# Forming the weight sums of five quads twice, in a projection kernel held by TensorE

## The chip, the cores and the metric

One core of a Trainium2 chip. The metric is the device time of one launch in microseconds, as the median of the runs shown.

## The reference

One layer of a hybrid decoder for 2048 new tokens of one sequence and 64 tokens of eight running ones (2112 rows of 1024 in all), in float32:

```python
xn = rms_norm(x, norm_pre)
z = einsum('btd,de->bte', xn, w_in)          # w_in: 1024 x 4096
v_pool, g_pool, u_lru, g_lru = four column blocks of z, 1024 wide each
y_pool = pool_mixer(v_pool)                  # causal means over 2/4/8/16 tokens, a 256x256 map per group, a scale
y_lru = rg_lru(causal_conv(u_lru))           # 4-tap convolution, two 128x128 gates per head, a linear scan over time
mixed = concat(y_pool * silu(g_pool), y_lru * silu(g_lru))
out = x + rms_norm(mixed @ w_out, norm_post)  # w_out: 2048 x 1024
```

Besides `out` the new states of the pool, the convolution and the scan are returned.

## The kernel before

**Tokens and quads.** The 2112 tokens are worked in three macro chunks of 704 (`m` = 0, 1, 2; `LM` = 2 is the last), each of two halves of 352. The 4096 columns of w_in are 16 quads per macro chunk, a quad `(m, p, kind)` being 256 columns: kind V (pool input), G (pool gate), U (lru input) or L (lru gate), p = 0 to 3. The order of p differs by macro chunk (`P_ORDER`); in the last third it is 1, 2, 3, 0. Every float32 operand is split into a high and a low part (fp32r), and a product takes three matmuls.

**Seven products for eight.** A quad is a 2 x 2 block product (two column blocks, two halves of the inner dimension) with two token halves. In the second and last third each quad is done with seven products in place of eight, the Strassen-Winograd way. The seven left operands carry numbers 1 to 7 (`pid`): 1, 2 and 4 are raw weight blocks ("11", "12", "22"), and 5, 7, 6, 3 are sums of them. The seven right operands are x or sums of x, and lie in `XN` under the names X11, T1, T2, X22, T3, X21, T4. One product is a *slot* of 12 matmuls of 352 columns in `quad_slot` (line 1127); the matmul's line is 267.

**Where weights come from.** All split operands of a quad go through tiles of one ring (`half_tile`, 7 buffers of 512 KB). A split operand is stored once to a DRAM scratch `wsd` by `hi_lo` (line 888, the store on line 898), and is read back by later macro chunks in `w_step` (line 980, load on line 984). In the second third a quad is *late* (`is_late`, line 763) if its sums do not exist yet: then `w_raw` (line 869) loads its four raw blocks (256 KB each, line 368) into the small rings `raw` and `tp`, `s_sum` (line 908) makes the sums in place on VectorE (lines 339 and 342), and each is cast on ScalarE (line 890) and subtracted on VectorE (line 339) into the ring, and stored. In the last third every operand is loaded from `wsd`.

**x for the next macro chunk.** `x_chain` (line 1415) loads token tiles (line 291) for the squares on ScalarE (line 307), then x itself, transposed, into the staging tiles `XA` and `XB` (line 1435), and scales it on VectorE (line 1457). `transition` (line 1471) then forms and splits the seven x operands out of the staging tiles.

**The order.** The program is written out by a planner: `one_slot` (line 1606) emits the matmuls of a slot and then, with `run_jobs`, whatever work of ScalarE ("A"), VectorE ("V") and GpSimd fits beside it by assumed durations; "t" in a job is a waiting time, "D" a DMA issue, "?" a condition. The result is one fixed order for each engine. Almost all DMAs are issued from the SyncE queue in the planner's order; the stores of `mixed` come from GpSimd. `prep` (line 1853) starts loads: raw blocks up to `RAW_AHEAD` = 14 slots before their quad, operands up to `AHEAD` = 6 slots. Each engine and each queue works in order, so an instruction that waits holds those behind it.

**After the projections.** `combos_chain` (line 1554) loads w_out, forms four sums of its blocks and stores them to DRAM (`wtd`), at a pace of 12 us for each of eight steps; `region_chain` (line 1579) loads and splits five pieces of w_out into tiles that take over the buffers of `XA` and `XB`, and spawns ahead of the sums. Both run during the last third. From about 805 us on the output projection runs over pairs of token tiles.

Of the kernel before, what the change touches and what calls it, by code (L numbers as in the profile page):

```python
# [25 lines left out]
LM = NM - 1  # L26
# [18 lines left out]
PIECE = 512  # L45
# [20 lines left out]
X0_LEAD = 3  # L66
FROM_P = 2
P_ORDER = ((0, 1, 2, 3), (2, 1, 3, 0), (1, 2, 3, 0))
TABLE_COST = 1.4
LAG = 4.0  # L70
WO_PACE = 12.0
# [1 line left out]
XL_ON = "V"  # L73
SG_ON = "V"
X_LEAD = (7, 10)
XOF_0 = {1: "X22", 5: "X11", 6: "T2", 3: "T4", 7: "T1", 2: "T3", 4: "A"}
ORDER_0 = (1, 5, 6, 3, 7, 2, 4)
XOF = {1: "X11", 6: "T2", 5: "T1", 7: "T3", 4: "T4", 2: "X21", 3: "X22"}
# [6 lines left out]
def hymba_kernel(  # L85
# [133 lines left out]
    def xa_tile(h, name, dtype=F32):  # L219
        return sb.tile([P, 2 * QW], dtype, tag=f"XA{h}", bufs=1, name=name)  # L220
# [143 lines left out]
    def blocks(kind, p):  # L364
        return [KINDS[kind] + 2 * p + j for j in range(2)]
# [392 lines left out]
    EARLY = "VG"  # L758

    def is_made(q):  # L760
        return q[0] == 0 and q[1] >= FROM_P and q[2] in EARLY

    def is_late(q):
        return q[0] == 1 and (q[1] < FROM_P or q[2] not in EARLY)

    w_tiles, w_rawt = {}, {}
    jobs, pe_q, clock, T = [], [], {"V": 0.0, "A": 0.0, "G": 0.0}, [0.0]
# [97 lines left out]
    PLAIN_PID = {"11": 1, "12": 2, "22": 4}  # L865
    S_OF = {5: "22", 6: "11", 7: "21", 3: "12"}
    w_time = {}

    def w_raw(q):
        _, p, kind = q  # L870
        w_time[q] = T[0] + 5.0
        for n in NAMES:
            blk, h = blocks(kind, p)[int(n[0]) - 1], int(n[1]) - 1
            t = (raw_tile if n[0] == "1" else tp_tile)(f"wr{q[0]}{kind}{p}_{n}")
            w_rawt[q, n] = w_load_raw(blk, h, t)

    def flat_of(t):
        return t.rearrange("p a b -> p (a b)")
# [9 lines left out]
    def hi_lo(hi, lo, src, store=None, key=None):  # L888
        yield "A", 0.62
        AC.copy(out=hi, in_=src)  # L890
        yield "V", 0.71
        tsub(lo, src, hi.bitcast(F32))
        if key:
            w_fin[key] = clock["V"] + HOP
        if store:
            yield "t", LAG
            yield "D", 0
            nc.sync.dma_start(out=w_key(*store[1:]), in_=store[0].bitcast(F32))

    w_jobs = {}  # L900
# [79 lines left out]
    def w_step(q, pid):  # L980
        m, p, kind = q
        t = w_tiles[q, pid] = half_tile(f"w{m}{kind}{p}_{pid}")
        if not is_late(q) or pid in (1, 2, 4):
            nc.sync.dma_start(out=flat_of(t).bitcast(F32), in_=w_key(kind, p, pid))
            return
        n = S_PID.index(pid)
        if n == 0:
            w_jobs[q, "s"] = {"n": 0, "job": spawn(s_sums(q, lambda i: w_jobs[q, "s"].update(n=i + 1)),
                                                        max(T[0], w_time[q]), rank=0,
                                                        due=lambda: w_first[q, S_PID[w_jobs[q, "s"]["n"]]] - 1)}  # L990
        box = w_jobs[q, "s"]

        def wait_split():
            yield "?", lambda: box["n"] > n
            yield from hi_lo(t[:, 0, :], t[:, 1, :], w_rawt[q, S_OF[pid]], (flat_of(t), kind, p, pid),
                             (q, pid))
        w_jobs[q, pid] = spawn(wait_split(), rank=0, due=lambda: w_first[q, pid])

    def need_w(q, n):
# [415 lines left out]
    def x_chain(m):  # L1415
        first = -(-m * MW // P)
        tiles = list(range(first, min(-(-(m + 1) * MW // P), N_TT)))
        places = [("B", 0), ("B", 1)] + ([("A", 0), ("A", 1)] if m > 1 else [])
        for i0 in range(0, len(tiles), len(places)):
            part = tiles[i0:i0 + len(places)]  # L1420
            for i, (s_, j) in zip(part, places):
                yield "D", 0
                load_tok(i, s_, j)
                yield "t", 3.0
            yield "t", 5.0
            for i in part:
                yield "A", 1.06
                tok_square(i)
        for h in (1, 0):
            if m == 1 and h == 0:  # L1430
                yield "?", lambda: x0_free
                x_tiles["A"] = xa_tile("A", "XA1")
            for k in range(0, HK, 2):
                yield "D", 0
                nc.sync.dma_start(out=stage_x(h)[:, k:k + 2, :],
                                  in_=xt[:, HK * h + k:HK * h + k + 2, m * MW:(m + 1) * MW])
                yield "t", 2.5
        yield "V", 0.2
        yield "A", 0.3, "sqrt"
        tok_rsqrt(tiles[0], tiles[-1] + 1)  # L1440
        clock["V"] = max(clock["V"], clock["A"]) + 0.5
        yield "t", 0.8
        yield "?", lambda: t_free() >= 2
        dg, rt = roots(m)
        for c in range(2):
            yield "A", 1.5
            r_diag(2 * m + c, dg[:, c * CW:(c + 1) * CW])
        for c in range(2):
            def rows(c=c):
                R = r_rows(2 * m + c, dg[:, c * CW:(c + 1) * CW])  # L1450
                return [("A", 0.45, lambda: AC.copy(out=rt[:, c * CW:(c + 1) * CW], in_=R))]
            yield "P", rows
        yield "t", 3.0
        for k in range(KT):
            yield "V", 0.92
            a = stage_x(k // HK)[:, k % HK, :]
            V.scalar_tensor_tensor(out=a, in0=a, scalar=col(C_NP, k), in1=rt[:, :MW], op0=ALU.mult, op1=ALU.mult)
        t_done(2)
        x_ready.add(m)
# [94 lines left out]
    def combos_chain():  # L1554
        def load(k):
            r = {}
            for i, j in ((0, 0), (1, 1), (0, 1), (1, 0)):
                r[i, j] = (raw_tile if i else tp_tile)(f"wo{k}_{i}{j}")
                nc.sync.dma_start(
                    out=r[i, j], in_=w_out[(8 * i + k) * P:(8 * i + k + 1) * P, PIECE * j:PIECE * (j + 1)])  # L1560
            return r
        nxt = load(0)
        yield "t", 6.0
        for k in range(KT):
            yield "D", 0
            r, nxt = nxt, load(k + 1) if k + 1 < KT else None
            for j, o, a, b in ((T1, (0, 0), (0, 1), (0, 0)), (T3, (0, 1), (1, 1), (0, 1)),
                               (T2, (1, 1), (1, 1), (0, 0)), (T4, (1, 0), (1, 0), (1, 1))):
                yield "V", 0.68
                tsub(r[o], r[a], r[b])  # L1570

                def store(j=j, k=k, o=r[o]):
                    yield "t", 2.0
                    yield "D", 0
                    nc.sync.dma_start(out=wtd[:, j, k, :], in_=o)
                spawn(store(), clock["V"] + HOP, rank=3)
            yield "t", WO_PACE

    def region_chain(r, j, k0, k1):
        yield "D", 0  # L1580
# [100 lines left out]
    with tc.manual_schedule():  # L1681
# [171 lines left out]
        def prep(n):  # L1853
            while raw_next[0] < len(raw_quads):
                q = raw_quads[raw_next[0]]
                if first_of[QUADS.index(q)] - n > RAW_AHEAD:
                    break
                if raw_next[0] > 1 and not raw_done(raw_quads[raw_next[0] - 2]):
                    break
                w_raw(q)  # L1860
                raw_next[0] += 1
            while w_next[0] < len(w_order):
                at, q, pid = w_order[w_next[0]]
                if at - n > AHEAD or (w_next[0] >= W_BUFS and w_last[w_order[w_next[0] - W_BUFS][1:]] > n):
                    break
                if (q[0] == 0 or is_late(q)) and q not in w_time:
                    break
                if q[0]:
                    w_step(q, pid)
                elif is_made(q):  # L1870
                    made_tile(q, pid)
                else:
                    plain_tile(q, pid)
                w_next[0] += 1
# [23 lines left out]
        for n, (qi, i, _, _) in enumerate(slots):  # L1898
            first_of.setdefault(qi, n)
        done = set()  # L1900
        first_made = min(qi for qi, q in enumerate(QUADS) if is_made(q))
        for n, (qi, i, qp, pid) in enumerate(slots):
            q = QUADS[qi]
# [15 lines left out]
                    0, ("X11", "T1", "T2", "A")[(len(x0_jobs) - 1) % 4]] - 2)  # L1919
            if m < LM and (qi, i) == (lasts[m] - X_LEAD[m], 0):  # L1920
                spawn(x_chain(m + 1), rank=0, due=lambda m=m: first_of[lasts[m]])
            if m == 2 and (qi, i) == (lasts[1] + 2, 0):
                spawn(region_chain(0, "b11", 0, 5), then=[lambda: spawn(combos_chain())])
                nc.sync.dma_start(out=stc, in_=st_conv)
                nc.sync.dma_start(out=stl, in_=st_lru)
            x_turn(n, qi)
# [23 lines left out]
        def p1_chain():  # L1950
# [10 lines left out]
            for g in range(5):  # L1961
                it = p1_slots(g)
                for part in range(3):
# [11 lines left out]
                            load_11(g + 4)  # L1975
                    yield [("A", 0.6, lambda g=g: p1_out(g))] if part == 2 else []

        spawn(region_chain(1, T3, 0, 8), rank=2)
        pc = p1_chain()
        for _ in range(15):  # L1980
# [132 lines left out]
```

## Time and profile before

| | us |
|---|---|
| median of 3 runs | 1149.36 |
| lowest and highest | 1147.45 and 1150.91 |
| profiled execution | 1153.73 |
| its span, first to last instruction | 1152.0 |
| second third of the tokens | about 293 to 547 |
| last third | about 547 to 805 |
| output projection | about 805 to the end |

In the profile PE is TensorE's matmul, PEld its weight load, DVE VectorE, ACT ScalarE, POOL GpSimd and SP SyncE. Tile names drop their numbers: `w1V` is a split weight operand of a V quad in the second third (`w2V`: last third), `wr1U` a raw block, `wsd` the scratch of split operands, `XAB` a staging tile of x, `lw` and `pw` the small maps, and `a1V`, `e1V`, `d1V` the three accumulators of a V quad in the second third. In rows of a timeline a bracket at the end gives the engine's idle time before the row and what ended it.

### The profile page before, as it was taken

How to read it: one execution, taken by the hardware profiler on the slowest of the kernel's cores; microseconds unless marked ns; L12 is line 12 of the kernel's file. 1: busy time of each engine (PE TensorE's matmuls, PEld its weight loads, DVE VectorE, ACT ScalarE, POOL GpSimd, SP SyncE). 2: the span in 40 equal slices, each digit the busy share in tenths (PEclk: the TensorE clock that was granted, in tenths of full speed). 3: DMA queues.
4: the chain of work that ended last, by engine and by line, in shares of the span. 5: the costliest groups of instructions: out<-in, count | busy, mean ns of one | idle time of the engine just before them, and what ended most of it. 6: DMA issues, size and time to landing. Idle time of an engine off the chain costs nothing. (4 is left out here: it accounts for less than half of the span.)

```text
span 1152.0 us, 17682 instructions
## 1 busy us (share of the span) xinstructions
PE 1119.7 (97%) x6226; PEld 1048.8 (91%) x6226; DVE 842.2 (73%) x1345; ACT 629.4 (55%) x1091; POOL 162.3 (14%) x264
## 2 busy tenths in 40 slices
PE   7999999999999989999999999999999999999996
PEld 5989999999999989999999999999888888888875
DVE  6798786768788657878787565645586678778777
ACT  4376778675676748458483636366663233344222
POOL 4200101002011100201011100201000012221232
PEclk9999999999999999999999999999999999999998
DMA  9655698885899998988999999987879567766553
GB/s 327 229 195 190 229 319 310 316 318 186 281 314 348 350 388 315 341 323 290 349 345 394 396 367 339 371 313 252 250 208 286 169 196 231 205 211 183 168 179 128
DMA packets 177464, 320.00 MB, mean 278 GB/s; under 512 B 24736, under 2 KB 86432, under 8 KB 177376
## 3 DMA queue, kind: packets, MB, share of 16 engines
q1 hardware_dynamic: 173536, 301.57, 76.4%
q0 software_dynamic: 3840, 17.30, 3.8%
q8 instruction: 49, 0.80, 0.3%
q14 instruction: 39, 0.32, 0.1%
HBM read 216.41 MB, written 102.15 MB: 277 GB/s over the span
## 5 line engine op out<-in xcount | busy, mean ns | idle before, releaser
L477 PE MATMUL p<-XN,s 128*128 128x512 f32 (+1 forms) x224 | 87.5, 391 | 2.1 <-DVE s L152 2.1
L475 PE MATMUL p<-XN,s 128*128 128x512 f32 (+1 forms) x224 | 87.4, 390 | 0.0
L476 PE MATMUL p<-XN,s 128*128 128x512 f32 (+1 forms) x224 | 87.3, 390 | 0.0
L1301 DVE SCALAR_TENSOR_TENSOR xs<-u,parT,xs 128x704 f32<-128x704 f32 (+1 forms) x72 | 66.8, 954 | 23.1 <-ACT xs L1290 22.9
L468 POOL TENSOR_TENSOR xr<-ac,xr 128x512 f32<-128x512 f32 x27 | 50.8, 1900 | 209.8 <-DVE ac L614 100.0
L269 PE MATMUL zL<-XN,wL 128*128 128x352 f32 x384 | 64.8, 325 | 0.6 <-DVE wL L339 0.6
L269 PEld LDWEIGHTS zL<-XN,wL 128*128 128x128 f32 x384 | 62.8, 188 | 0.8 <-DVE wL L339 0.8
L593 ACT ACTIVATE p<-ac 128x512 f32<-128x512 f32 (+1 forms) x32 | 18.8, 587 | 81.7 <-DVE ac L468 81.7
L468 DVE TENSOR_TENSOR a<-a,a 128x512 f32<-128x512 f32 x48 | 32.9, 690 | 37.2 <-DMA a<-mixed 34.5
L160 ACT ACT_TABLE_LOAD x46 | 59.0, 1283 | 1.5 <-PEq L2092 0.8
L149 ACT CAST s<-a 128x512 fp32r<-128x512 f32 x48 | 28.6, 616 | 53.5 <-DVE a L468 40.6
L1273 POOL DMA_DIRECT2D mixed<-g x24 | 13.2, 549 | 296.1 <-ACT g L1105 59.7
L476 PE MATMUL p<-XN,a 128*128 128x512 f32 x137 | 54.2, 396 | 0.0
L475 PE MATMUL p<-XN,a 128*128 128x512 f32 x137 | 54.2, 395 | 0.0
L477 PE MATMUL p<-XN,a 128*128 128x512 f32 x137 | 54.2, 395 | 0.0
L269 PE MATMUL y<-dh,pw 128*128 128x352 f32 x192 | 54.1, 323 | 0.0
L477 PEld LDWEIGHTS p<-XN,s 128*128 128x128 f32 x224 | 42.4, 189 | 12.1 <-DVE s L152 2.6
L476 PEld LDWEIGHTS p<-XN,s 128*128 128x128 f32 x224 | 42.5, 190 | 9.6
L475 PEld LDWEIGHTS p<-XN,s 128*128 128x128 f32 x224 | 42.5, 190 | 9.6
L269 PE MATMUL zU<-XN,wU 128*128 128x352 f32 x288 | 48.0, 325 | 0.0
L269 PEld LDWEIGHTS zU<-XN,wU 128*128 128x128 f32 x288 | 46.9, 188 | 0.0
L1264 DVE SCALAR_TENSOR_TENSOR g<-y,parT,g 128x352 f32<-128x352 f32 x48 | 27.9, 580 | 25.0 <-PE y L269 24.8
(407 smaller groups left out, 3140.4 us busy)
## 6 DMA issues: line engine op xcount, KB each, us to landing
a<-mixed SPq DMA_DIRECT2D x112, 256.0 KB, 4.1
mixed<-g POOLq DMA_DIRECT2D x48, 352.0 KB, 5.7
w2V<-wsd SPq DMA_DIRECT2D x28, 512.0 KB, 7.4
w2G<-wsd SPq DMA_DIRECT2D x28, 512.0 KB, 7.5
w2U<-wsd SPq DMA_DIRECT2D x28, 512.0 KB, 7.8
w2L<-wsd SPq DMA_DIRECT2D x28, 512.0 KB, 7.7
w1V<-wsd SPq DMA_DIRECT2D x20, 512.0 KB, 5.6
w1G<-wsd SPq DMA_DIRECT2D x20, 512.0 KB, 7.4
```

What stands on the lines that cost most here:

```text
L149: hi_eng.copy(out=hi, in_=src)
L160: nc.scalar.preload_act_table_set(name)
L269: nc.tensor.matmul(out, lhsT=lhsT, rhs=rhs, start=start, stop=stop)
L468: (eng or nc.vector).tensor_tensor(out=out, in0=a, in1=b, op=op)
L475: nc.tensor.matmul(out, lhsT=ah, rhs=wh, start=start and k == 0, stop=False)
L476: nc.tensor.matmul(out, lhsT=ah, rhs=wl, start=False, stop=False)
L477: nc.tensor.matmul(out, lhsT=al, rhs=wh, start=False, stop=stop and k == KT - 1)
L593: nc.scalar.activation(out=junk, in_=o, func=AF.Square, accum_out=st[:, g:g + 1])
L1264: V.scalar_tensor_tensor(out=g[:, cs], in0=Y, scalar=col(C_SCALE, blk), in1=g[:, cs], op0=ALU.mult, op1=ALU.mult)
L1273: nc.gpsimd.dma_start(out=mixed[:, blk, m * MW:(m + 1) * MW], in_=g[:, :MW])
L1301: V.scalar_tensor_tensor(out=xs, in0=E[:, k:k + n], scalar=col(C_CW + 8 * k, b), in1=xs, op0=ALU.mult, op1=ALU.add)
```

## The change

It has four parts.

1. `REMADE` names five quads: (1,"U"), (1,"L"), (2,"U"), (3,"U"), (3,"L"). In the last third they are late too: their four raw blocks are loaded again, now into the staging tiles of x (`XR1` to `XR5`, alternately in the buffers of `XB` and `XA`), and the sums 5, 7, 6 and 3 are formed and split again. Operands 1, 2 and 4 are still loaded from `wsd`. The sums of these quads are no longer stored in the second third. Raw loads of the last third wait until the transition to it is over (`x_jobs` empty).
2. The due time of the next sum is that of the earliest use among the sums not yet made, for all late quads.
3. The pace of the x loads is 3.0 us for the second third (before, 3.0 for tokens and 2.5 for x) and 7.0 for the last (before the same 3.0 and 2.5).
4. Since the raw blocks use the buffers of `XA` and `XB` until the last remade quad is done, `region_chain` is spawned only then, and `combos_chain` at its old place.

```diff
+REMADE = ((1, "U"), (1, "L"), (2, "U"), (3, "U"), (3, "L"))
...
+X_PACE = (3.0, 7.0)
...
     def is_late(q):
-        return q[0] == 1 and (q[1] < FROM_P or q[2] not in EARLY)
+        return q[0] == 1 and (q[1] < FROM_P or q[2] not in EARLY) or q[0] == 2 and q[1:] in REMADE
...
     def w_raw(q):
         _, p, kind = q
         w_time[q] = T[0] + 5.0
-        for n in NAMES:
+        if q[0] == LM:
+            n_xr[0] += 1
+            xr = xa_tile("AB"[n_xr[0] % 2], f"XR{n_xr[0]}")
+        for i, n in enumerate(NAMES):
             blk, h = blocks(kind, p)[int(n[0]) - 1], int(n[1]) - 1
+            if q[0] == LM:
+                w_rawt[q, n] = w_load_raw(blk, h, xr[:, PIECE * i:PIECE * (i + 1)])
+                continue
...
-                                                        due=lambda: w_first[q, S_PID[w_jobs[q, "s"]["n"]]] - 1)}
+                                                        due=lambda: min(w_first[q, o] for o in S_PID[w_jobs[q, "s"]["n"]:]) - 1)}
...
-            yield from hi_lo(t[:, 0, :], t[:, 1, :], w_rawt[q, S_OF[pid]], (flat_of(t), kind, p, pid),
-                             (q, pid))
+            store = None if (p, kind) in REMADE else (flat_of(t), kind, p, pid)
+            yield from hi_lo(t[:, 0, :], t[:, 1, :], w_rawt[q, S_OF[pid]], store, (q, pid))
...
                 load_tok(i, s_, j)
-                yield "t", 3.0
+                yield "t", X_PACE[m - 1]
...
-                yield "t", 2.5
+                yield "t", X_PACE[m - 1]
...
+                if q[0] == LM and (begun[0] < LM or x_jobs):
+                    break
                 w_raw(q)
...
+            if m == LM and not wo_begun and combos_done and raw_next[0] == len(raw_quads) and all(raw_done(q_) for q_ in raw_quads):
+                wo_begun.append(n)
+                spawn(region_chain(0, "b11", 0, 5))
             if m == 2 and (qi, i) == (lasts[1] + 2, 0):
-                spawn(region_chain(0, "b11", 0, 5), then=[lambda: spawn(combos_chain())])
+                spawn(combos_chain())
```

`combos_done` is set at the end of `combos_chain`.

More of the change, by code (lines that the diff above doesn't have):

```diff
@@ L867, in hymba_kernel @@
     w_time = {}
+    n_xr = [0]
     def w_raw(q):
@@ L1577, in combos_chain @@
             yield "t", WO_PACE
+        combos_done.append(True)
+    combos_done = []
     def region_chain(r, j, k0, k1):
@@ L1900, in hymba_kernel @@
         done = set()
+        wo_begun = []
         first_made = min(qi for qi, q in enumerate(QUADS) if is_made(q))
@@ L1976, in p1_chain @@
                     yield [("A", 0.6, lambda g=g: p1_out(g))] if part == 2 else []
+        assert wo_begun
         spawn(region_chain(1, T3, 0, 8), rank=2)
```

## The prediction

> **What bounds the kernel now.** I read the page first, then the waits of TensorE, then the windows of the last two thirds of the tokens, then the timeline of TensorE around each wait.
>
> ```profile
> span 1152.0 us, 17682 instructions
> ...
> PE 1119.7 (97%) x6226; PEld 1048.8 (91%) x6226; DVE 842.2 (73%) x1345; ACT 629.4 (55%) x1091; POOL 162.3 (14%) x264
> ```
>
> TensorE is the bound: 97% of the span, and nothing in the change takes a matmul away. So only holes in its stream can be won. This is the waits view of TensorE between 96 and 1104 us (total, times, longest):
>
> ```profile
> PE r L269 <- DMA lw<-swd: 2.0, 2, 1.3
> PE a1V L267 <- DMA w1V<-wsd: 1.8, 1, 1.8
> PE a2L L267 <- DMA w2L<-wsd: 1.7, 1, 1.7
> PE e1V L267 <- DMA w1V<-wsd: 1.6, 1, 1.6
> PE a2V L267 <- DVE XN L339: 0.9, 1, 0.9
> PE a1U L267 <- ACT u L1105: 0.9, 1, 0.9
> PE e2L L267 <- ACT g L1105: 0.6, 1, 0.6
> ```
>
> Seven lines, 9.5 us in all, 7.1 of them ended by a DMA: that is the whole field. The windows show where (PE, PEld, DVE, ACT, POOL busy; clock; DMA share; GB/s). The second third of the tokens runs from about 293 to 547 us, the last from 547 to 805.
>
> ```profile
> 369.30:410.00 40.70, 39.23 (x242) 38.94 (x240) 22.18 (x32) 29.10 (x46) 3.19 (x10) 1.00 0.96 355
> 410.00:430.00 20.00, 18.14 (x100) 17.64 (x101) 13.66 (x23) 9.61 (x17) 1.56 (x2) 0.91 1.01 384
> 430.00:547.60 117.60, 116.74 (x721) 116.27 (x721) 95.87 (x136) 78.04 (x127) 13.99 (x26) 1.00 0.89 319
> 547.60:618.00 70.40, 68.63 (x421) 68.05 (x419) 55.67 (x79) 40.11 (x67) 9.72 (x22) 1.00 0.98 352
> 618.00:660.00 42.00, 41.56 (x254) 41.32 (x255) 26.47 (x44) 25.12 (x39) 6.44 (x13) 1.00 1.03 401
> 711.00:805.00 94.00, 94.00 (x580) 94.00 (x579) 54.23 (x90) 48.45 (x82) 11.24 (x32) 1.00 0.89 325
> ```
>
> The DMA engines are full (0.96 to 1.03) exactly where TensorE waits; where they have a tenth to spare (711 to 805) it does not wait at all. The largest hole, in TensorE's timeline:
>
> ```profile
> 404.46 2.12 PE L267 MATMUL a1U<-XN,w1U 128*128 128x352 f32 x12
> 406.42 2.11 PE L267 MATMUL a1V<-XN,w1V 128*128 128x352 f32 x12
> 410.08 2.18 PE L267 MATMUL e1V<-XN,w1V 128*128 128x352 f32 x12 [1.55 <-DMA w1V<-wsd]
> 412.25 2.21 PE L267 MATMUL d1V<-XN,w1V 128*128 128x352 f32 x12
> 416.23 3.68 PE L267 MATMUL a1V<-XN,w1V 128*128 128x352 f32 x12 [1.78 <-DMA w1V<-wsd]
> 419.71 2.17 PE L267 MATMUL a1G<-XN,w1G 128*128 128x352 f32 x12
> ```
>
> An undisturbed slot of 12 matmuls takes 406.42 - 404.46 = 1.96 us. The four slots from 406.42 to 419.71 took 13.29 instead of 7.84: the hole costs 5.45 us, of which 3.33 is idle and the rest slow restart (the last slot took 3.48; the clock in its window was 0.91). The other five DMA and engine waits stand alone and cost little over their idle time; with about a tenth each, everything that could be won is some 13 us, 10 of it behind DMAs.
>
> **The hole's cause.** SyncE's issues before it, then what stood on ScalarE and VectorE:
>
> ```profile
> 395.03 0.32 SPq L984 DMA_DIRECT2D w1V<-wsd  x1
> 395.44 0.46 SPq L291 DMA_DIRECT2D XAB<-in_x  x1
> 396.30 0.32 SPq L984 DMA_DIRECT2D w1V<-wsd  x1
> 398.70 5.61 SPq L368 DMA_DIRECT2D wr1L<-in_w_in  x4
> 408.29 1.06 ACT L307 ACTIVATE XAB<-XAB 128x1024 f32<-128x1024 f32 x1 [1.22 <-DMA XAB<-in_x]
> 410.42 0.95 DVE L1301 SCALAR_TENSOR_TENSOR xs<-u,parT,xs 128x704 f32<-128x704 f32 x1 [9.16 <-ACT xs L1290]
> ```
>
> A weight load issued at 395 or 396 us released TensorE at 410: some 14 us. Loads of x stand between the weight loads in the one SyncE queue, and ScalarE, which works in order, waited for one of them (408.29), with VectorE idle 9.16 us behind it.
>
> **The change part by part.** (1) Stores. Five quads times four sums of 512 KB are no longer stored in the second third: 10 MB less written. (2) Loads. In the last third the same 20 loads of 512 KB go, and 20 raw loads of 256 KB come: 5 MB less. Together 15 of 320 MB. (3) x for the last third: 7 us between loads instead of 3.0 and 2.5. Six token tiles and four pieces of x: by the code, 6 x 4 + 4 x 4.5 = 42 us longer.
>
> For the hole, parts 1 and 3 count. Quad (1,"U") stood just before it, so four stores go, 2 MB or 5.5 us at that window's 384 GB/s; the last two token tiles (1 MB, 2.7 us) move from 395-397 to about 404 and 411. The weight loads then come some 8 us sooner, against waits of 1.55 and 1.78. I take the whole **-5.5**; the ends are -5.5 and 0 (if another load takes that place).
>
> What part 3 endangers is the end of x's preparation, which must be done before the last quad of the second third:
>
> ```profile
> 472.37 0.94 DVE L1457 SCALAR_TENSOR_TENSOR XAB<-XAB,parT,rt 128x704 f32<-128x704 f32 x1
> 533.85 2.12 PE L267 MATMUL a1L<-XN,w1L 128*128 128x352 f32 x12
> ```
>
> The last scaling ended at 473, so there are 60 us and 42 are used: 515, 18 us to spare. VectorE has 95.87 of 117.60 us busy in that stretch and the eight scalings only move within it. I take 0; if the cover went, each us late is a us of TensorE, up to 5.
>
> (4) The work of remaking. Rows of the same work in the second third:
>
> ```profile
> L339 DVE TENSOR_TENSOR w1U<-wr1U,w1U 128x512 fp32r<-128x512 f32 x16 | 11.0, 688 | 10.6 <-ACT w1U L890 7.4 <-DMA wr1V<-in_w_in 3.1
> L339 DVE TENSOR_TENSOR wr1U<-wr1U,wr1U 128x512 f32<-128x512 f32 x12 | 8.3, 689 | 0.2
> L890 ACT CAST w1U<-wr1U 128x512 fp32r<-128x512 f32 x16 | 9.9, 617 | 10.0 <-PE d1L L267 5.7 <-DMA wsd<-w1L 3.3 <-PE e1G L267 1.0
> DMA to landing us min/median/max: 3.4/5.7/10.6
> ```
>
> 20 sums and 20 differences are 20 x 0.689 + 20 x 0.688 = 27.5 us of VectorE; 20 casts 12.3 us of ScalarE. The windows leave VectorE some 15 us of air from 547 to 618, 15 more to 660 and 40 from 711 to 805: the work fits beside the matmuls. What it costs is order: more evacuations come late. All engine-ended waits of TensorE above are 0.9 + 0.9 + 0.6 = 2.4 us in the two thirds, with VectorE as busy in the second third as it will now be in the last. I take **+0.5**, ends 0 and 2.4.
>
> (5) The first remade quad, (1,"U"). Its raw loads go into the staging buffer of x, which is free only once the last x operand (T4) is split, so they are issued about slot 9 of the last third, and its sums are wanted five or six slots later. Every other remade quad has 14 slots.
>
> ```profile
> 568.24 2.12 PE L267 MATMUL a2V<-XN,w2V 128*128 128x352 f32 x12
> 581.87 2.12 PE L267 MATMUL e2U<-XN,w2U 128*128 128x352 f32 x12
> 608.74 0.48 SPq L1029 DMA_DIRECT2D lw<-swd  x1
> 688.25 0.34 SPq L1192 DMA_DIRECT2D out<-op  x1
> 697.35 0.34 SPq L1192 DMA_DIRECT2D out<-op  x1
> ```
>
> The first slot with T4 is that at 568.24, the first with a sum that at 581.87. Sum, cast and difference take 0.69 + 0.62 + 0.69 = 2.0 us and some tenths of handing over, so the raw words must land by 579.3, 11 us after their issue. The row above has 5.7 as median and 10.6 as worst in the second third, and a full queue adds to it. VectorE, in order, stands at the sum until they land, and behind it the evacuations. I take **+0.8**, ends 0 and 8: a lateness of 5 us, at the hole's rate of 5.45 for 3.33 idle.
>
> (6) Combinations of w_out start about 15 us sooner (the five splits of its first region go out of their way to the end of the stage), and the raw loads of the next two quads come 14 slots ahead. Both crowd the queue before 608.74, where lw is issued, whose first wait is 1.3 us; ends -1.3 and +4, I take **+0.5** since the loads of sums that go (eight before 618 and soon after) pay for most of it. The second lw wait, 0.8 at 680, is behind eight more loads that have gone: **-0.9** with its restart, ends -0.9 and 0. The wait of 1.7 us of a2L comes after SyncE stood 9.1 us (688.25 to 697.35) at a state output that waits for a small buffer; that quad is not remade and nothing here moves it: 0, ends -1.9 and +1.7.
>
> (7) The moved region splits: 5 x (0.62 + 0.69) us, in a stretch (711 to 805) with ScalarE 48.45 and VectorE 54.23 of 94 busy. 0; without this cover 6.6 us ahead of the first output product.
>
> Sum: -5.5 + 0.5 + 0.8 + 0.5 - 0.9 = **-4.6 us**. The profiled execution took 1153.73 us (span 1152.0 and 1.7 around it), 4.4 above the median of 1149.36, so it comes to 1149.1, and the median to **1144.8**.
>
> [...] The hole's last slot ran at about half speed after idle times of 1.55 and 1.78. [...]
>
> **The rivals.** *All DMA waits go* (1139 to 1141): the two lw waits and that of a2L go with the hole, 5.5 + 1.8 + 1.0 + 1.9 = 10.2 us. For it: 15 MB less in full windows. Against: the 9 us stand of SyncE stays, and the combinations come sooner.
> *The first remade sum comes late* (slower, 1153 to 1155): raw loads of (1,"U") take as long as the 14 us seen at 395, so they land 3 us or more too late and VectorE holds its evacuations with it. Price up to 8 us, and the same crowd at lw up to 3.5 more; it turns the result to slower from about 8 us in all. Against: 11 us are there.
> *Given back* (1148 to 1151): the hole goes, and the last third loses 4 to 5 us over several small waits, of raw sums, lw and evacuations.
> *No hole to fill in ordinary runs* (1147 to 1149): the profiled execution is 4.4 us longer than the median, and a hole behind a full DMA queue is just what profiling may have deepened. Then the change wins 1 or 2.
>
> **How the numbers follow.** Chances: forecast 0.45 (own range 1142 to 1147), all DMA waits 0.12, late first sum 0.17, given back 0.14, no hole 0.12. About 0.3% (3.4 us) is what this measurement can tell from no change: 1145.9 and 1152.8. Of the forecast 0.36 lies below, so faster 0.36 + 0.12 = 0.48; slower 0.17; same 0.35. The range 1139.5 to 1152.5 leaves out most of the late-sum case and little else.
>
> **What would show it.** Right: no DMA wait of TensorE between 400 and 420, clock 1.00 there, no stand of ScalarE at a token tile, some 305 MB moved, VectorE about 27 us busier from 547 to 805. Wrong: a wait at the first sum of (1,"U") after 575, a longer wait for lw near 618, idle TensorE just before the last third, or the hole at another weight load of the second third.

## The result, and the profile after

| kernel | median, us | lowest and highest | ratio to before, 95% interval |
|---|---|---|---|
| before, run beside it on the same chip | 1150.91 | 1147.38 and 1155.16 | |
| changed | 1159.68 | 1152.24 and 1163.77 | 1.0068 [1.0043, 1.0093] |

The change makes the kernel slower by 0.7%, 8.8 us between the medians; forecast were 1144.8 and at most 1152.5. The profiled execution below is the shortest of its thirteen (1152.24 us), so its rows show less than the typical loss; a second profile of it (e7, 1159.54 us) stands further on. The mean granted clock was 0.995 to 0.998 in the four shortest executions (up to 1154.73 us) and 0.989 to 0.993 in the nine others (from 1158.45 us).

From the page of the changed kernel, TensorE's busy time and the traffic:

```profile
span 1150.5 us, 17678 instructions
...
PE 1116.7 (97%) x6226; PEld 1046.0 (91%) x6226; DVE 867.3 (75%) x1385; ACT 639.4 (56%) x1110; POOL 162.1 (14%) x264
...
DMA packets 174585, 304.28 MB, mean 264 GB/s; under 512 B 24416, under 2 KB 86112, under 8 KB 174496
```

The windows of the changed kernel, in the columns of those shown of before (time, PE, PEld, DVE, ACT, POOL busy with counts; clock; DMA share; GB/s):

```profile
410.00:430.00 20.00, 20.00 (x126) 20.00 (x125) 18.07 (x26) 9.93 (x19) 2.85 (x4) 1.00 0.96 329
547.00:618.00 71.00, 66.77 (x404) 65.03 (x403) 55.13 (x79) 36.21 (x60) 9.10 (x22) 1.00 0.96 344
618.00:660.00 42.00, 38.65 (x237) 38.09 (x236) 27.71 (x47) 16.55 (x33) 1.84 (x9) 1.00 0.85 291
```

The hole of the second third is gone: 126 matmuls from 410 to 430 where there were 100, at clock 1.00. From 618 to 660 the changed kernel did 237 where the kernel before did 254. The boundaries of the stages show the same. First the row that opens the last third and the first output products before, then the same of the changed kernel (the first from TensorE's timeline, the second from the view of tile `p`: count, duration, first and last start):

```profile
547.57 1.14 PE L267 MATMUL a2V<-XN,w2V 128*128 128x352 f32 x6
...
L269 PE MATMUL p<-X2A,a x10: 392/396/442, 806.0 to 814.9; 128*128 128x512 f32 x10
```

```profile
540.17 2.12 PE L269 MATMUL a2V<-XN,w2V 128*128 128x352 f32 x12
...
L271 PE MATMUL p<-X2A,a x10: 392/397/502, 805.2 to 814.9; 128*128 128x512 f32 x10
```

The last third began 7.4 us earlier and ended only 0.8 us earlier: 258.4 us before, 265.0 now. The gain was made, and 6.6 us of it were given back in the very stage that remakes the sums. All waits of TensorE in that stage sum to 12.1 us here and to 5.3 before, so what was given back is idle time. In e7 the two marks are 542.46 and 809.4, 266.9 us.

Where it went, in TensorE's timeline of the changed kernel (in brackets the idle time and what ended it):

```profile
580.20 2.62 PE L269 MATMUL a2U<-XN,w2U 128*128 128x352 f32 x12 [1.30 <-ACT w2U L899]
604.43 2.19 PE L269 MATMUL a2V<-XN,w2V 128*128 128x352 f32 x12 [1.14 <-DMA w2V<-wsd]
614.09 2.18 PE L269 MATMUL a2G<-XN,w2G 128*128 128x352 f32 x12 [0.66 <-DMA w2G<-wsd]
619.93 2.21 PE L269 MATMUL d2G<-XN,w2G 128*128 128x352 f32 x12 [0.71 <-DMA w2G<-wsd]
624.78 2.19 PE L269 MATMUL a2G<-XN,w2G 128*128 128x352 f32 x12 [2.64 <-DMA w2G<-wsd]
675.97 2.19 PE L269 MATMUL a2V<-XN,w2V 128*128 128x352 f32 x12 [1.20 <-DMA w2V<-wsd]
689.47 2.19 PE L269 MATMUL a2G<-XN,w2G 128*128 128x352 f32 x12 [1.52 <-DMA w2G<-wsd]
```

One wait is for a remade sum (1.30, for the cast of (1,"U")'s first). The other six, 7.87 us in all, are for loads of *ready* operands of V and G quads, which the change does not remake; four of them, 5.15 us, lie before 630 us. No wait for `lw` is among them. Three waits at the very end of the stage are new too: 0.73 us for a `g` of VectorE at 800.88, and 1.18 us for ScalarE and 0.54 us for VectorE at the first output products. No run tests what brought them; e4, with all five quads, has only the last.

What stood in front of these loads, in SyncE's timeline of the changed kernel (start, time spent issuing):

```profile
557.08 2.06 SPq L1568 DMA_DIRECT2D wo<-in_w_out  x4
562.89 2.63 SPq L370 DMA_DIRECT2D XR<-in_w_in  x4
566.30 2.30 SPq L1568 DMA_DIRECT2D wo<-in_w_out  x4
...
592.71 5.27 SPq L370 DMA_DIRECT2D XR<-in_w_in  x4
...
601.96 0.50 SPq L1038 DMA_DIRECT2D lw<-swd  x1
603.08 1.60 SPq L993 DMA_DIRECT2D w2G<-wsd  x2
604.98 3.45 SPq L1568 DMA_DIRECT2D wo<-in_w_out  x4
...
612.31 4.61 SPq L370 DMA_DIRECT2D XR<-in_w_in  x4
617.33 0.33 SPq L993 DMA_DIRECT2D w2G<-wsd  x1
```

In the kernel before the first `wo` load was issued here:

```profile
582.96 2.52 SPq L1559 DMA_DIRECT2D wo<-in_w_out  x4
```

So the combinations of w_out started 25.9 us earlier than before, not 15, and the raw blocks of (1,"L") (592.71) and (2,"U") (612.31) were issued in the middle of them, 14 slots before their quads. The `w2G` load at 617.33, behind four raw loads, released TensorE at 624.78, 7.5 us later and 2.64 late. It landed 7.3 us after its issue, about the median of such loads before (7.5), so it was late because it was issued late; the one at 610.42, which TensorE awaited 0.71 us at 619.93, was slow as well (9.5).

### The profile page after: what moved, and what is told of

It reads as the page before. It is cut to its first block, busy times and chain, and to the rows that moved or that the text cites. A ratio compares the mean times of both kernels' runs of the same rounds, so it can differ in the third digit from the quotient of the medians.

```text
span 1150.5 us, 17678 instructions
## 1 busy us (share of the span) xinstructions
PE 1116.7 (97%) x6226; PEld 1046.0 (91%) x6226; DVE 867.3 (75%) x1385; ACT 639.4 (56%) x1110; POOL 162.1 (14%) x264
## 2 busy tenths in 40 slices
DMA packets 174585, 304.28 MB, mean 264 GB/s; under 512 B 24416, under 2 KB 86112, under 8 KB 174496
## 5 line engine op out<-in xcount | busy, mean ns | idle before, releaser
L470 POOL TENSOR_TENSOR xr<-ac,xr 128x512 f32<-128x512 f32 x27 | 46.7, 1749 | 211.1 <-issue 106.3
```

Source lines behind the costliest of these rows:

```text
L470: (eng or nc.vector).tensor_tensor(out=out, in0=a, in1=b, op=op)
```

## The experiments

All ratios are to the kernel before, run beside it on the same chip; differences between two kernels are differences of their ratios times 1150 us.

| label | remade | combinations start | other edit | median, us | ratio, 95% interval |
|---|---|---|---|---|---|
| e1_pace_alone | none, order of before | before | pace | 1147.75 | 0.9968 [0.9951, 0.9985] |
| e2_nothing_remade | none | early | | 1155.86 | 1.0029 [1.0010, 1.0049] |
| e3_old_pace | five | early | old pace | 1155.02 | 1.0034 [1.0014, 1.0054] |
| e4_combos_later | five | a quad later | | 1153.42 | 1.0002 [0.9983, 1.0020] |
| e5_two_remade | (3,"U"), (3,"L") | later | | 1146.04 | 0.9965 [0.9943, 0.9987] |
| e6_order_only_later | none | later | | 1148.13 | 0.9997 [0.9975, 1.0019] |
| e8_first_and_last | (1,"U") and the two of e5 | later | | 1148.83 | 1.0002 [0.9983, 1.0021] |
| e9_without_first | all but (1,"U") | later | | 1152.51 | 1.0037 [1.0009, 1.0065] |
| e10_region_waits | none | later | casts 5 us later | 1143.22 | 0.9958 [0.9937, 0.9979] |
| e11_two_region_waits | as e5 | later | casts 5 us later | 1149.59 | 1.0012 [0.9993, 1.0031] |
| e12_second_state_tile | none | later | as e10, second `op` tile | 1142.66 | 0.9943 [0.9923, 0.9963] |
| e13_raw_loads_closer | five | early | raw loads 8 slots ahead | 1151.51 | 1.0024 [1.0004, 1.0045] |
| e14_pace_and_state_tile | none, order of before | before | pace, second `op` tile | 1142.87 | 0.9942 [0.9922, 0.9962] |
| e15_all_five_mended | five | later | edits of e12 and e13 | 1144.35 | 0.9957 [0.9938, 0.9975] |

**Theory and rivals.** My theory after the result: the queue before 630 us is crowded, by combinations that start too early and raw loads that come too early. Rivals: the extra work of VectorE and ScalarE for the remade sums; the late first sum of (1,"U"); the new order at the end of the stage, with no remaking in it at all.

### The parts one by one: e1 to e4

e1 is the kernel before with the new pace of the x loads alone; nothing is remade and the old stores stay.

```diff
+X_PACE = (3.0, 7.0)
-                yield "t", 3.0
+                yield "t", X_PACE[m - 1]
...
-                yield "t", 2.5
+                yield "t", X_PACE[m - 1]
```

> The kernel before with only the wider pace of the x loads (3.0 and 7.0 us); nothing remade, nothing reordered in the last third. Crowd theory (the loss sits in the SyncE queue of the last third, the gain in the second third): the wait for w1V near 410 us goes or shrinks under 1 us, and the time is 2 to 5 us below the kernel before. Pace theory (the wider pace itself costs, by late x): slower than before by 3 us or more, with idle TensorE before the last third.

e2 is the changed kernel with `REMADE = ()`: the new pace and the new order of the combinations and the region stay.

> The changed kernel with an empty list of remade quads: pace, due times and the order of the w_out work as changed, all operands of the last third loaded and all sums stored. Crowd theory in the form that the earlier w_out combinations are to blame: slower than before by 4 to 9 us, with DMA waits of TensorE between 560 and 640 us. Remaking theory (the sums formed again hold up VectorE and ScalarE and the raw loads crowd the queue): as fast as the pace alone, 2 to 5 us below the kernel before.

e3 is the changed kernel with the old waits of 3.0 and 2.5 us in the x loads.

> The changed kernel with the old pace of the x loads (3.0 and 2.5). If the pace closed the hole at 410 us, it comes back: 4 to 6 us above the changed kernel (about 1164). If the stores that are gone closed it, no more than 2 us of difference. If the pace costs, faster than the changed kernel.

e4 is the changed kernel with `combos_chain` spawned one quad later.

```diff
+            if m == 2 and (qi, i) == (lasts[1] + 3, 0):
+                spawn(combos_chain())
             if m == 2 and (qi, i) == (lasts[1] + 2, 0):
-                spawn(combos_chain())
```

> The changed kernel with the w_out combinations begun one quad later (some 16 us, about where they began in the kernel before). Crowd theory: 3 to 6 us below the changed kernel (1154 to 1157), with fewer DMA waits between 600 and 630 us. Remaking theory: within 2 us of the changed kernel.

The windows of the whole second third, of before, e1 and e3 in turn:

```profile
293.00:547.00 254.00, 249.82 (x1526) 248.55 (x1526) 194.35 (x276) 166.58 (x266) 28.09 (x56) 0.99 0.91 329
```

```profile
293.00:547.00 254.00, 253.90 (x1564) 253.43 (x1563) 199.55 (x282) 169.31 (x271) 30.77 (x56) 1.00 0.93 336
```

```profile
293.00:547.00 254.00, 254.00 (x1567) 253.78 (x1566) 200.86 (x283) 170.03 (x271) 28.54 (x56) 1.00 0.84 297
```

The pace alone (e1) closes the hole, and so does what e3 keeps at the old pace: the stores that go, with the new due times, which no run takes apart. In time the pace alone is worth 0.32%, 3.7 us, with an interval from 1.7 to 5.6. e3 holds a miss: it is 3.9 us faster than the changed kernel (intervals overlapping), which was named beforehand as the sign of a pace that costs. Its profile does not show where (its first output products begin at 808.1 us, against 805.2 in the changed kernel), and this stays open.

e2 puts the loss elsewhere: with no sum remade, the new order turns the pace's gain into 1.0029, 7.0 us above e1. Remaking adds 4.5 us (e2 to the changed kernel, intervals overlapping slightly). Starting the combinations a quad later takes 7.6 us off the changed kernel (e4, intervals apart), more than the 3 to 6 expected, so their early start, beside these raw loads, is most of its loss; in e4 they start at 572.18, still 10.8 us before the kernel before. In e4's profile TensorE has one wait left between 580 and 640 us, 2.62 us at 616.19; the profile names ScalarE's `xh`, but a `w2G` load issued at 605.36 landed 10.7 us later, just before TensorE went on.

e2's own 7.0 us are mostly something else. Load waits between 560 and 640 us were expected there; its profile has 1.6 us of them. TensorE's waits in the last third sum to 12.2 us in e2 and 5.2 in e1, and 5.0 of the difference stand from 729 to 740 us behind casts of the moved region (ScalarE's first such cast, then the longest of TensorE's three waits):

```profile
728.94 0.62 ACT L1599 CAST X2A<-wb 128x512 fp32r<-128x512 f32 x1 [12.32 <-DMA wb<-in_w_out]
...
734.69 2.22 PE L269 MATMUL e2V<-XN,w2V 128*128 128x352 f32 x12 [2.51 <-ACT e L1114]
```

So the new order has two costs: the combinations that start early beside the raw loads (e4), and the casts of the region at the end of the stage (this profile). e10 below tests the second.

### Which quads, and the later order without them: e5, e6, e8, e9

All four are e4 with another list (e6: `REMADE = ()`).

```diff
-REMADE = ((1, "U"), (1, "L"), (2, "U"), (3, "U"), (3, "L"))
+REMADE = ((3, "U"), (3, "L"))                                  # e5
+REMADE = ((1, "U"), (3, "U"), (3, "L"))                        # e8
+REMADE = ((1, "L"), (2, "U"), (3, "U"), (3, "L"))              # e9
```

> The changed kernel with the w_out combinations one quad later and only the last two quads of the list, (3,U) and (3,L), remade: the raw loads of (1,U), (1,L) and (2,U) leave the stretch 560 to 617 us and their 12 loads of sums come back up to 650. If the raw loads 14 slots ahead crowd the first half of the last third: 3 to 5 us below the run with combinations later alone (1148 to 1150), with no wait over 2 us before 625. If the remaking costs through VectorE and ScalarE in proportion to the quads: 2 us below it. If remaking costs nothing: no difference.

> The changed kernel with nothing remade and the w_out combinations one quad later: what is left of the change is the pace, the due times and the region splits at the end of the stage. If the earlier combinations cost 7 us with or without remaking: 1147 to 1149, like the pace alone, and 7 to 9 us below the same kernel with the combinations early. If the region splits at the end cost: 3 us or more above the pace alone.

> As the run with two remade quads (combinations one quad later), with (1,U) remade as well: the quad whose raw loads have only five or six slots. If its late first sum is what remaking costs: 2 to 4 us above the run with two (ratio 0.998 to 1.000), with a wait of TensorE near 580 us. If the raw loads of (1,L) and (2,U) in the full queue of 589 to 617 us are: no more than 1 us above it.

> As the run with two remade quads, with (1,L) and (2,U) remade as well and (1,U) not. If the raw loads of these two in the full queue cost: 3 to 5 us above the run with two (about 1.000), with DMA waits of TensorE for w2V or w2G between 600 and 630 us. If (1,U) is what costs: no more than 1 us above it.

None 0.9997, the two late quads 0.9965, those and (1,"U") 1.0002, all but (1,"U") 1.0037, all five 1.0002. No cost of the two late quads is seen; their raw loads stand, in SyncE's timeline of e5, at

```profile
673.45 2.88 SPq L370 DMA_DIRECT2D XR<-in_w_in  x4
...
703.46 1.85 SPq L370 DMA_DIRECT2D XR<-in_w_in  x4
```

and not in the stretch before 630. e9 against e5 puts 8.3 us on (1,"L") and (2,"U") with intervals apart; its waits for loads, in TensorE's timeline:

```profile
604.51 2.18 PE L269 MATMUL a2V<-XN,w2V 128*128 128x352 f32 x12 [1.79 <-DMA w2V<-wsd]
611.91 2.19 PE L269 MATMUL a2V<-XN,w2V 128*128 128x352 f32 x12 [1.33 <-DMA w2V<-wsd]
704.42 3.86 PE L269 MATMUL a2L<-XN,w2L 128*128 128x352 f32 x12 [4.02 <-DMA w2L<-wsd]
```

All are for loads of ready operands, none for a sum; one more, 1.74 us at 765.30, is for an evacuation while ScalarE stands 3.98 us at a cast of the region. (1,"U") costs too (e8 against e5, 4.3 us, intervals overlapping by 0.0004), though no wait of e8 is at its first sum, where one was expected; its longest is 3.38 us for a `w2L` load at 700.82. The numbers do not add up quad by quad: all five take less than four. Each list gives the planner another order of everything, and no single-quad price should be read from this row.

### The end of the stage: e10 and e11

e6 should have kept all of e1's gain (0.9968) and did not: it is 3.7 us faster than e2 (intervals overlapping) where 7 to 9 were expected. ScalarE's and TensorE's timelines of e6:

```profile
761.38 0.62 ACT L1599 CAST X2B<-wb 128x512 fp32r<-128x512 f32 x1 [6.37 <-DMA wb<-in_w_out]
```

```profile
762.41 3.89 PE L269 MATMUL a2U<-XN,w2U 128*128 128x352 f32 x12 [4.68 <-ACT u L1114]
766.09 2.37 PE L269 MATMUL e2U<-XN,w2U 128*128 128x352 f32 x12
```

ScalarE stands 6.37 us at the cast of a piece of w_out that has not landed (its load was issued at 753.33 and took 8.0 us), and the evacuation `u` queued behind it keeps an accumulator from TensorE for 4.68 us. The next slot took 3.68 us (766.09 - 762.41) in place of 1.96. e10 and e11 are e6 and e5 with 5 us more before the cast of each piece of this region:

```diff
+            if r == 0:
+                yield "t", 5.0
```

> As the run with nothing remade and combinations later, with 5 us more between the load of each piece of the first w_out region and its cast, which the planner spends on other work of ScalarE. If the cast that waits for its load holds up ScalarE and through the evacuations behind it TensorE (4.7 us near 762 us in that run): the wait goes, 4 to 6 us less, ratio 0.994 to 0.996. If the wait has another cause: it stays within 1 us.

> As the run with two remade quads, with the same 5 us between load and cast of the first region. In that run ScalarE stood 7.6 us at those casts and TensorE did not wait there, so by the profile no gain: 0.995 to 0.998. If ordinary executions do wait there: 2 us or more below the run with two.

e10 gains 4.5 us over e6 (intervals overlapping by 0.0004) and has no wait of TensorE between 707 and 805; the longest stand of ScalarE at these pieces is

```profile
753.26 0.62 ACT L1601 CAST X2A<-wb 128x512 fp32r<-128x512 f32 x1 [1.15 <-DMA wb<-in_w_out]
```

e11 was expected to keep or better e5's 0.9965 and came to 1.0012: a miss. In e5 the casts had not held TensorE, so there was nothing to win. Why 5.4 us were lost (intervals apart) stays open: the profile of e11 shows three larger new waits, 0.93 us for `w2G` at 685.56, 2.08 for `w2L` at 698.64 and 2.03 of the first output products for ScalarE at 802, but e5's 2.41 for `lw` and 0.94 for `pw` have shrunk to 0.33 in all, and the span (1147.5) is only 2.1 us above that of e5 (1145.4).

### The queue's own stands: e12 and e13

In e10 SyncE still stood some 6 us at the store `out<-op` near 690 us, as in the kernel before. e12 is e10 with a second buffer for that tile; e13 is the changed kernel with its raw loads 8 slots ahead.

```diff
-                op = sb.tile([P, N_S + 1, PB], F32, tag="op", bufs=1, name=f"op{blk}")
+                op = sb.tile([P, N_S + 1, PB], F32, tag="op", bufs=2, name=f"op{blk}")
...
-                if first_of[QUADS.index(q)] - n > RAW_AHEAD:
+                if first_of[QUADS.index(q)] - n > (8 if q[0] == LM else RAW_AHEAD):
```

> e10 (the new order, nothing remade, the combinations later, the region's first casts 5 us later) with a second buffer for the state output's tile, so that SyncE no longer stands some 6 us for it near 690 us. If this standing is what keeps the w2L load back and TensorE waiting near 700 us: the standing gone, that wait under 1 us, 1 to 3 us less than e10, a ratio of 0.993 to 0.995. If the queue is late for its own transfers: the wait near 700 us stays, and 0.995 to 0.997 as e10.

> The changed kernel with the raw weights' loads of the five quads made 8 slots ahead in place of 14, nothing else moved. If the raw loads stand in front of the w2G and w2V loads between 575 and 630 us: those waits shrink, 1 to 4 us less than the changed kernel, a ratio of 1.003 to 1.006. If only the earlier combinations matter: no difference, 1.006 to 1.008; if the loads now come too late for the sums, a wait of TensorE on ScalarE's w2U or w2G grows, and it is above 1.008.

SyncE's issues from that tile in e10 and in e12, from the views of the tile (first and last start):

```profile
L1201 SPq DMA_DIRECT2D out<-op x2: 337/340/344, 687.7 to 695.5; - x2
```

```profile
L1201 SPq DMA_DIRECT2D out<-op x2: 338/341/344, 680.0 to 683.7; - x2
```

7.8 us apart in e10, 3.7 in e12, and the last third of e12 reads

```profile
547.00:805.00 258.00, 256.21 (x1558) 253.68 (x1557) 167.20 (x258) 141.78 (x232) 43.10 (x83) 1.00 0.96 351
```

with 1.2 us of waits in all and none near 700. In e10 these waits come to 6.4 us, 3.4 of them for `w2V` and `w2G` between 606 and 616, so the second buffer may help at more places than the one near 700. The stand is shown to go; in time the step from e10 is 1.7 us, within the intervals.

e13 took 5.1 us off the changed kernel (the intervals touch), a little more than expected. In its SyncE timeline the raw loads of (1,"L") have moved from 592.71 to

```profile
605.22 6.39 SPq L370 DMA_DIRECT2D XR<-in_w_in  x4
```

and of the six waits for `w2V` and `w2G` two are left, 1.27 us at 674 and 3.73 at 620. So the raw loads' lead carries its own part of the crowd.

### What the two ideas are worth when nothing is in the way: e14 and e15

e14 is e1 with the second `op` buffer; e15 is e4 (all five remade) with the 5 us before the casts, the second `op` buffer and the lead of 8.

> The kernel before with two edits alone: the pace of the x loads (3 and 7 us) and a second buffer for the state output's tile. If these two, the hole at 410 us and the queue's standing near 690 us, are what could be won: 0.993 to 0.996, below the pace alone (0.9968), with no wait of TensorE near 700 us. If the later order of the last third is needed too: 0.996 to 0.999, the waits for lw near 610 and 680 us staying.

> All five quads remade, as in the changed kernel, with everything mended that the runs named: combinations later, raw loads 8 slots ahead, the region's first casts 5 us later, two buffers for the state output's tile. If nothing is left against remaking but the crowd in the queue: 0.993 to 0.996, as the same order with nothing remade (0.9943), 6 to 8 us less than with all five and the combinations later alone. If remaking itself costs, by its work on VectorE and ScalarE in order: 0.998 to 1.002, with waits of TensorE that ScalarE or VectorE ended.

The waits of TensorE between 96 and 1104 us in e14, then in e15:

```profile
PE r L270 <- DMA lw<-swd: 1.5, 2, 1.1
PE a2V L268 <- DVE XN L340: 1.0, 2, 0.8
```

```profile
PE d2G L269 <- DMA w2G<-wsd: 1.7, 1, 1.7
PE a2L L269 <- DMA w2L<-wsd: 1.2, 1, 1.2
PE a2V L269 <- DVE XN L341: 1.0, 2, 0.8
PE p L271 <- DVE a L154: 0.6, 1, 0.6
PE a2V L269 <- DMA w2V<-wsd: 0.2, 1, 0.2
```

With all five quads remade and the queue in order, e15 is 12.8 us faster than the changed kernel (0.9957 against 1.0068). What is left of remaking is at most small: 1.6 us above e12, which remakes nothing, within the intervals. But it buys nothing either: e14, two small edits of the kernel before, reaches 0.9942, as fast as any kernel here, at 1142.87 us. Its two waits for `lw` stayed, which had been named as the sign that more was needed.

### The changed kernel a second time: e7

> The changed kernel once more, for a second profile: the first one caught 1152 us where the median is 1160. If a typical execution loses its 8 us in the last third: matmuls counted there fall by 30 to 50 more, with waits over 2 us and a granted clock below 1.00 in stretches between 600 and 720. If it loses them elsewhere (the output projection): the last third counts as in the first profile.

The windows of the first profile and then of e7, which runs the same program 7.3 us longer (1159.54 and 1152.24):

```profile
72.00:96.00 24.00, 21.56 (x132) 21.02 (x131) 21.86 (x30) 15.57 (x27) 0.22 (x2) 1.00 0.56 201
620.00:640.00 20.00, 17.36 (x105) 17.10 (x106) 13.76 (x22) 9.21 (x16) 0.97 (x6) 1.00 0.88 316
547.00:805.00 258.00, 246.02 (x1496) 242.61 (x1494) 182.62 (x286) 140.28 (x233) 34.06 (x82) 1.00 0.92 319
```

```profile
72.00:96.00 24.00, 21.53 (x114) 20.99 (x113) 20.25 (x28) 14.09 (x23) 0.22 (x2) 0.86 0.51 184
620.00:640.00 20.00, 16.83 (x93) 16.26 (x92) 13.19 (x22) 8.74 (x16) 1.43 (x6) 0.91 0.88 313
547.00:805.00 258.00, 246.94 (x1492) 243.44 (x1490) 181.54 (x284) 138.54 (x230) 35.10 (x82) 0.99 0.91 321
```

I had expected 30 to 50 matmuls fewer in the last third; there are 4 fewer, so the gap between profile and median is not one place that went wrong. Of the 7.2 us between the two spans, 2.3 arise before the last third, 1.9 in it and 3.0 after it. e7 waits at the same operands, and in some places the clock then falls and in the first profile it did not (0.86 and 0.91 against 1.00 in the rows above).

## Why the prediction was wrong

**The step that failed: (6), the crowd in the queue.** I took +0.5 with ends of -1.3 and +4. Three things in it were wrong. The combinations came 25.9 us sooner, not 15: I counted the splits that go out of their way, not where the planner would then put each load. I looked for the loss at `lw` alone, because its wait was the one in the trace; in the changed kernel `lw` is issued sooner (601.96 against 608.74) and lands in time, and the loads of V and G operands became the late ones. And I let the loads that go pay for those that come, by bytes, from the reading that TensorE waits where the DMA engines are full. That does not hold: the last third of e12 moves 351 GB/s at a DMA share of 0.96 with 1.2 us of waits, that of the changed kernel 319 GB/s at 0.92 with some 12. What stands in front of a load counts as well. Measured: 7.87 us of idle time in six waits, and by experiment 7.6 us from the combinations' start (e4) or 5.1 from the raw loads' lead (e13). These two are not a sum, since each clears the same queue.

**From profile to median.** I put the 4.4 us by which the profiled execution lay above its median on both kernels. Between the two profiles the change came out 1.5 us faster (1152.24 and 1153.73) where -4.6 was forecast; the medians came out 8.8 us the other way, because the profile before lies 2.8 us above the median beside it and that of the changed kernel 7.4 below its own. The rows above therefore show a part of the loss; that the order makes it is shown by the medians of e4, e13 and e15.

**Step (7), the region's splits,** was costed at 0 because ScalarE and VectorE are half idle there (busy 48.45 and 54.23 of 94 us before). In the changed kernel TensorE indeed loses nothing to them, though ScalarE stands 6.48 us at one piece. But the reason was wrong: e2 lost 5.0 us and e6 4.68 us of idle time there, and e10 won 4.5 of e6's back. In e6 a cast that waited 6.37 us for its load kept ScalarE from the evacuation behind it, though ScalarE was busy for only 136 of the stage's 258 us.

**The hole, -5.5,** was right in place, cause and cure; by e1 it is 3.7 us [1.7, 5.6] in ordinary executions. That 7.4 us came out between the profiles is luck in part: a wait of 0.86 us for a `u` at 524.98 went too, and from 72 to 96 us the clock was 1.00 in place of 0.93 (132 matmuls for 126). One reading beside the cause was too large: ScalarE stood 1.22 us at the token tile, so at most that much of VectorE's 9.16 us lay behind it. The rival of no hole in ordinary runs fell; that the profiled execution shows the hole deeper than usual is possible but not shown, since 5.45 lies within the interval.

**Parts that held.** Traffic: 304.28 MB for some 305. x's end: no wait at the end of the second third. The extra work (4): VectorE 867.3 for 842.2 us, and of the waits for it only 0.73 us for a `g` and 0.54 us at the output products are new. The first remade sum (5): wanted at 580.20 (I had 581.87), 1.30 us of idle time for the +0.8 taken, so the rival of the late sum has little support in the profile, though e8 against e5 leaves it up to some 4 us. (4) and (5) together were +1.3; e15 against e12 gives 1.6, within the intervals. The second `lw` wait went, as taken.

**The a2L wait.** I read 9.1 us of SyncE standing at the state output out of the two stores at 688.25 and 697.35. A load lies between them, so the stand is 6.0 us, from 691.40 to 697.35:

```profile
691.07 0.33 SPq L984 DMA_DIRECT2D w2L<-wsd  x1
```

I put 0 on it since nothing of the change moves it, and passed on. No wait for that load is in the changed kernel's profile; one near 700 us was in most kernels with the combinations later (1.20 in e15 still). A second buffer takes the stand away: e14 over e1 is 3.0 us, within the intervals.

Of the rivals, *given back* had the form (several small waits in the last third that eat the hole's gain) with 4 to 5 us for it, but named raw sums, `lw` and evacuations as what is awaited; the loss was about 12 (8.8 between the medians and 3.7 of gain). My one case for slower put most of the loss on the first remade sum, on the engine that does the new work, and the rest at `lw`, not on the loads of ready operands that share the queue.

## What to carry to other kernels

Traffic saved was not time saved here, where one queue feeds the bound engine (304.28 MB moved for 320.00, and 8.8 us more time): list what the change puts in front of each load that the engine waits for, with its issue time, and price it by queue place, and not by bytes alone. Where a change lets a background job start sooner, take its new start from the order itself: starting sooner cost 7.6 us here (the changed kernel against e4), in a stretch with a DMA share of 0.96 (547 to 618 us). A queue or engine that stands some microseconds at one small buffer is worth an edit of its own: a second buffer and a slower pace for x together made a kernel as fast as any here (e14, 0.9942), without the large change. And one profile is one execution: set its time against the median before a forecast is built on the difference.

## What the runs showed of the hardware

**The clock fell after short waits, and not each time.** Two executions of the changed kernel wait at the same place near 81 us. From 72 to 96 us the first did 132 matmuls at clock 1.00 after a wait of 1.75 us, and e7 114 at 0.86 after 1.79 (each then waited 0.69 us more). In the last third the first profile had its longest wait, 2.64 us at 624.78, with clock 1.00 over 620 to 640; e7 fell to 0.91 there with waits of 1.27 us at 622.33 and of 1.90:

```profile
626.41 2.87 PE L269 MATMUL a2G<-XN,w2G 128*128 128x352 f32 x12 [1.90 <-DMA w2G<-wsd]
```

So waits of about the same length cost their idle time in one execution and some 1.4 to 2.9 us more in another (12 and 18 matmuls fewer, at 1.96/12 us each, less the 0.5 us that TensorE idled longer in the window of the 12), which fits a spread of 11.5 us between executions of one program and their mean clocks of 0.989 to 0.998. No wait in these windows is longer than the 2.64 us after which the clock stayed at 1.00; what decides whether it falls is not shown.

**The same issue took from 1.85 to 6.39 us.** Four raw loads took SyncE 1.85 us to issue at 703.46 in e5, 2.63 at 562.89 and 5.27 at 592.71 in the changed kernel, and 6.39 at 605.22 in e13, and what is behind them waits: the `w2G` load at 617.33 was issued 0.4 us after four that took 4.61. In the changed kernel the DMA share does not explain it (1.06 from 562 to 566, around the 2.63, 0.94 from 592 to 598, around the 5.27, and 1.03 from 612 to 617, around the 4.61); what does is not shown.
